# The first stage of a two-layer decoder trunk in another order: row parameters in one load, the first weights in two parts, work moved between ScalarE, VectorE and GpSimd

## The chip, the cores and the metric

The kernel runs on 1 core of one Trainium2 chip. Its time is device microseconds from start to end of one launch; lower is better. TensorE (PE in the profile) multiplies matrices, VectorE (DVE) and ScalarE (ACT) work element by element and reduce, GpSimd (POOL) does small operations, and SyncE (SP) issues nearly all loads. Each engine takes its instructions in the order in which the program gives them; a semaphore makes one wait for another.

## The reference

256 tokens of width 1024 go through two layers. Layer 0 mixes tokens with multi-head latent attention, layer 1 with block attention and a relative bias; a squared-ReLU MLP of width 4096 follows each. All is float32. The part that matters here is the entry of layer 0:

```python
h = rms_norm(x, attn_norm[0])
proj = h @ w_in                                   # 1024 -> 384 + 256 + 64
c_q, c_kv, k_pe = proj[..., :384], proj[..., 384:640], proj[..., 640:]
q = rms_norm(c_q, q_a_norm) @ w_uq                # 8 heads x (128 + 64)
kv = rms_norm(c_kv, kv_a_norm) @ w_ukv            # 8 heads x (128 + 128)
q_nope, k_nope = rms_norm(q[:128]), rms_norm(kv[:128])
q_pe = rope(rms_norm(q[128:]), cos, sin)          # cos, sin of positions * inv_freq
k_pe = rope(rms_norm(k_pe), cos, sin)
p = softmax(causal((q_nope . k_nope + q_pe . k_pe) / sqrt(192)))
```

## The kernel before

A float32 product is made of three products of operands that are split into a high and a low part: high by high, low by high, high by low. Weights come as units of up to 128 x 1024. `load_one` (L130) issues a unit's load on SP, `hi` (L140) casts its high part (`wh`) on ACT (L148), `lo` (L150) subtracts it on DVE for the low part (`wl`, L157). Seven units are split ahead at most (`RING`), and four raw tiles are in flight (`RAW`); `done` tells how far PE has come. The order of instructions on every engine is the order of the source: the program is scheduled by hand.

The first stage is the projection by `w_in`. Its eight units of 128 x 704 (slices k = 0 to 7, named `win0` to `win7`) each need a piece of x, transposed, in the tile `x`: `make_h` (L252) makes the high part `hTh` on ACT and the low part `hTl` on DVE. PE runs slices 0 to 5 as they come, into four PSUM tiles (`latk` for the key and value latent of 256 + 64 columns, `latq` for the query latent of 384, one of each for the two token blocks), and then `lat_end` (L421) does slices 6 and 7, one tile after the other, so that `ckv` can be copied and transposed (L452) while `latq` is still being summed. The units of `w_u` (tile `raw`) follow: keys `k0`, the rope part of the queries `p`, queries `q0`, values `v0`, then the second four heads. `hi()` and `lo()` calls stand between these steps.

Beside it run: the rope angles (`rope_angles`, L365) on POOL from positions `pos_q` and the row `rowc` (inverse frequencies and two gain rows), the sines on ACT (L437), the rope tables on POOL (`rope_tables`, L388); the sums of squares of the token rows `xs` on DVE (L462), which give the scales; the roots `hrs` of the norms on POOL (L245); rows multiplied by them on DVE (L339); the two rope products of `rope_rows` (L735), one on POOL (L739) and one on DVE (L740), and their sums (L746). `turn0` transposes the finished rows on PE (L347). An activation of one element loads ACT's table for Exp (L758) before it is needed in the softmax. The first `logits` end the stage.

SP's loads at the start go in this order: slice 0, x, slice 1, x, `pos_q`, `rowc` (one row broadcast to 128 partitions), slice 2, x, slice 3 and so on, two units of `w_u`, then both halves of `xs`.

Of the kernel before, what the change touches and what calls it, by code (L numbers as in the profile page):

```python
# [59 lines left out]
def trunk(ctx: ExitStack, tc: tile.TileContext, A, out):  # L60
# [304 lines left out]
    def rope_angles(eng):  # L365
        eng.tensor_copy(posf, pos_q)
        for t in range(NT):
            eng.tensor_scalar(ang[:, t], rowc[:, :HALF], posf[:, t:t + 1], None, op0=OP.mult)
        for j, shift in enumerate((0.25, 0.0)):
            kk = mla.tile([P, NT, HALF], F32, name=f"kk{j}")  # L370
            eng.tensor_scalar(kk, ang, 1.0 / TWO_PI, shift, op0=OP.mult, op1=OP.add)
            eng.tensor_scalar(kk, kk, MAGIC, None, op0=OP.add)  # L372
            eng.tensor_scalar(kk, kk, MAGIC, None, op0=OP.subtract)  # L373
            rr = mla.tile([P, NT, HALF], F32, name=f"rr{j}")
            pr = mla.tile([P, NT, HALF], F32, name=f"pr{j}")
            src = ang
            for c in (C1, C2, C3):
# [2 lines left out]
                src = rr  # L380
            if j == 0:
                eng.tensor_scalar(rr, rr, TWO_PI / 4, None, op0=OP.add)
            eng.tensor_scalar(rr, rr, 3.1415925, -3.1415925, op0=OP.min, op1=OP.max)  # L383
            angles.append(rr)
# [741 lines left out]
```

## Time and profile before

| | |
|---|---|
| median of 3 runs | 581.11 us (579.84 to 581.11) |
| the profiled execution | 581.29 us |
| its span, first to last instruction | 579.5 us |
| PE busy | 567.9 us (98%) |
| DVE busy | 406.6 us (70%) |
| ACT busy | 307.0 us (53%) |
| POOL busy | 115.8 us (20%) |
| read from HBM | 97.79 MB, 171 GB/s over the span |

The shares are means over the whole span. The change lies in the first 52 us, in which all engines wait for one another; after that PE works nearly without a break. A row of a timeline gives the start in us from the span's start, the duration (of several instructions of a kind together), the engine, the line of the source, the operation, the tiles written and read, and in brackets the idle time before it with what ended it.

### The profile page before, as it was taken

The page shows a single profiled execution, that of the slowest core. Times are in us where ns is not written, and L with a number is a line of the kernel's source. Part 1 is how long each engine was busy: PE and PEld are TensorE (multiplying, and loading weights), DVE is VectorE, ACT ScalarE, POOL GpSimd, SP SyncE. Part 2 cuts the span into 40 slices and gives each one's busy share as a digit, 9 for nine tenths or more (in the row PEclk, how much of TensorE's full clock was granted, in tenths as well). Part 3 has the DMA queues.
Part 4 walks back from the last instruction along what each step waited for, and adds up shares of the span by engine and source line. Part 5 has one row for each costly group of instructions (what it writes and reads, how often), then busy time and mean ns, then how long its engine had stood idle before and what let it go on. Part 6 is the DMA issues. An engine that isn't in the chain of part 4 may idle for free.

```text
span 579.5 us, 10767 instructions
## 1 busy us (share of the span) xinstructions
PE 567.9 (98%) x4346; PEld 541.0 (93%) x4346; DVE 406.6 (70%) x646; ACT 307.0 (53%) x492; POOL 115.8 (20%) x119
## 2 busy tenths in 40 slices
PE   7899999999999999999999999999999999999997
PEld 5767999999999999999988888999999999999996
DVE  5696877678899987786648456776778554756641
ACT  5787775655433364643545555756664433555420
POOL 5884100022122200024324100000131222000100
PEclk9998999999999999999999999999999999999999
DMA  7732535555655656575654554345466666465630
GB/s 282 287 92 74 178 112 151 190 186 170 206 167 157 187 168 208 159 235 185 202 177 126 191 187 127 133 146 163 152 189 199 204 183 184 149 210 163 237 125 28
DMA packets 29265, 99.54 MB, mean 172 GB/s; under 512 B 4032, under 2 KB 4672, under 8 KB 29216
## 3 DMA queue, kind: packets, MB, share of 16 engines
q1 hardware_dynamic: 28736, 97.92, 52.9%
q0 software_dynamic: 336, 0.92, 0.4%
q8 instruction: 34, 0.56, 0.4%
q14 instruction: 15, 0.12, 0.1%
q10 hardware_dynamic: 144, 0.02, 0.0%
HBM read 97.79 MB, written 1.05 MB: 171 GB/s over the span
## 4 chain that ended last, share of the span: by engine, by line
PE 92%; POOL 4%; DVE 1%; DMA 1%; issue 1%; SPq 0%; ACT 0%; POOLq 0%
PE ps L84 90%; POOL hrs L245 1%; PE ps L347 1%; PE ps L544 1%; DMA rowc<-in_rowc 1%; POOL pr L378 1%; POOL rr L379 1%; POOL t L739 0%; POOL kk L373 0%; POOL kk L372 0%; DVE sqj L462 0%; DVE cqT L469 0%; DVE wl L157 0%; POOL scl L245 0%; POOL rr L383 0%
## 5 line engine op out<-in xcount | busy, mean ns | idle before, releaser
L148 ACT CAST wh<-raw 128x1024 fp32r<-128x1024 f32 x177 | 183.5, 1047 | 111.5 <-DMA raw<-in_w_out_mlp 58.3
L157 DVE TENSOR_TENSOR wl<-raw,wh 128x1024 fp32r<-128x1024 f32 x177 | 228.1, 1318 | 8.8 <-ACT wh L148 8.6
L84 PE MATMUL ps<-a,wh 128*128 128x256 f32 x1024 | 183.5, 280 | 0.0
L84 PEld LDWEIGHTS ps<-a,wh 128*128 128x128 f32 x1024 | 157.2, 188 | 0.0
L84 PE MATMUL ps<-hTh,wh 128*128 128x256 f32 x512 | 143.8, 281 | 0.0
L84 PE MATMUL ps<-hTh,wl 128*128 128x256 f32 x512 | 143.1, 279 | 0.0
L84 PE MATMUL ps<-a,wl 128*128 128x256 f32 x512 | 142.9, 279 | 0.0
L84 PE MATMUL ps<-hTl,wh 128*128 128x256 f32 x512 | 142.8, 279 | 0.0
L84 PEld LDWEIGHTS ps<-hTh,wh 128*128 128x128 f32 x512 | 96.2, 188 | 0.1
L84 PEld LDWEIGHTS ps<-hTl,wh 128*128 128x128 f32 x512 | 96.0, 188 | 0.0
L84 PEld LDWEIGHTS ps<-hTh,wl 128*128 128x128 f32 x512 | 95.9, 187 | 0.1
L84 PEld LDWEIGHTS ps<-a,wl 128*128 128x128 f32 x512 | 95.8, 187 | 0.0
L84 PE MATMUL ps<-aT,wh 128*128 128x256 f32 x256 | 51.0, 289 | 0.0
L84 PE MATMUL ps<-wh,hTh 128*128 128x512 f32 (+2 forms) x128 | 45.9, 387 | 1.9 <-ACT wh L148 1.7
L909 POOL TENSOR_TENSOR x<-t,x 128x256 f32<-128x256 f32 x16 | 26.4, 1649 | 94.7 <-DVE t L907 94.7
L84 PE MATMUL ps<-wh,hTl 128*128 128x512 f32 (+2 forms) x128 | 44.6, 376 | 0.0
L84 PE MATMUL ps<-wl,hTh 128*128 128x512 f32 (+2 forms) x128 | 44.6, 376 | 0.0
L873 DVE SCALAR_TENSOR_TENSOR t<-ps,t 128x512 f32<-128x512 f32 (+1 forms) x34 | 22.4, 658 | 28.0 <-ACT t L871 28.0
L907 DVE TENSOR_TENSOR t<-ps,scale 128x256 f32<-128x256 f32 x32 | 13.5, 421 | 38.9 <-PE ps L84 38.9
L84 PEld LDWEIGHTS ps<-aT,wh 128*128 128x128 f32 x256 | 40.5, 188 | 0.2
L876 DVE TENSOR_TENSOR a<-t,a 128x512 fp32r<-128x512 f32 (+1 forms) x34 | 22.5, 661 | 22.5 <-ACT a L875 22.5
L245 POOL TENSOR_TENSOR hrs<-hss,mhalf 128x4 f32<-128x4 f32 (+1 forms) x18 | 24.9, 1390 | 65.8 <-DVE hss L322 48.9
(157 smaller groups left out, 653.1 us busy)
## 6 DMA issues: line engine op xcount, KB each, us to landing
raw<-in_w_in_mlp SPq DMA_DIRECT2D x64, 512.0 KB, 3.9
raw<-in_w_out_mlp SPq DMA_DIRECT2D x64, 512.0 KB, 3.8
raw<-in_w_qkv SPq DMA_DIRECT2D x24, 512.0 KB, 3.8
raw<-in_w_u SPq DMA_DIRECT2D x8, 512.0 KB, 6.1
win<-in_w_in SPq DMA_DIRECT2D x8, 352.0 KB, 5.2
raw<-in_w_o0a SPq DMA_DIRECT2D x4, 512.0 KB, 3.6
raw<-in_w_o0b SPq DMA_DIRECT2D x4, 512.0 KB, 3.4
raw<-in_w_o1a SPq DMA_DIRECT2D x4, 512.0 KB, 4.0
```

What stands on the lines that cost most here:

```text
L84: nc.tensor.matmul(o, a, b, start=start, stop=stop)
L148: (eng.copy if eng is nc.scalar else eng.tensor_copy)(his[i][:, :w], raws[i][:, :w])
L157: eng.tensor_sub(los[i][:, :w], raws[i][:, :w], f32(his[i][:, :w]))
L245: nc.gpsimd.tensor_tensor(dst, t, mhalf[:, :n].rearrange("p (a b) -> p a b", b=t.shape[-1]) if len(t.shape) == 3 else mhalf[:, :n], op=OP.pow)
L347: nc.tensor.transpose(pt[:, i * P:(i + 1) * P], yf[:, i * P:(i + 1) * P], ident)
L378: eng.tensor_scalar(pr, kk, c, None, op0=OP.mult)
L379: eng.tensor_sub(rr, src, pr)
L544: nc.tensor.transpose(pt[:, i * P:(i + 1) * P], self.p[:, i * P:(i + 1) * P], ident)
L873: nc.vector.scalar_tensor_tensor(sq, src, 0.0, rl, op0=OP.max, op1=OP.mult)
L876: nc.vector.tensor_sub(al, sq, f32(ah))
L907: nc.vector.tensor_tensor(y, o, scale, op=OP.mult)
L909: nc.gpsimd.tensor_add(x[:, d], y, x[:, d])
```

## The change

It changes the order of the first stage and the engines of a few operations. The two small loads become one: `rowp`, 162 words for each of 128 partitions, holds the row parameters already repeated, and the two positions of that partition. It is loaded after slice 3. Slice 0 is loaded in two parts, first the 320 columns of `latk`, then the 384 of `latq`; DVE casts the first part, ACT the second, and PE runs slice 0 as six products of 320 columns and then six of 384. The first half of `xs` is loaded before the units of `w_u`, the second after two of them. The sum of squares of the first half goes from DVE to ACT, ahead of the cast of slice 7. Of the angles, the second set (j = 1) goes from POOL to DVE, with a fused multiply and subtract, two steps at a time after the low parts of slices 3 to 6. The sines and rope tables come after the second copy of `cq`. `hi` and `lo` of three units move up by a step. Exp's table load moves from behind the latents to behind the first key transposition, the rope product of L739 goes from POOL to DVE, and the second `rope_rows` moves behind it.

```diff
+RC = HALF + 2 * PE_D
@@ load_one
-        nc.sync.dma_start(raw[:, :n], src)
+        c = slice(QR if i == 0 else 0, n)
+        nc.sync.dma_start(raw[:, c], src[:, c])
@@
-    pos_q = const.tile([P, NT], I32)
-    rowc = const.tile([P, HALF + 2 * PE_D], F32)
+    rowp = const.tile([P, RC + NT], I32)
+    rowc, pos_q = f32(rowp[:, :RC]), rowp[:, RC:]
@@
-        if k == 1:
-            nc.sync.dma_start(pos_q, A["pos_col"])
-            nc.sync.dma_start(rowc, A["rowc"].to_broadcast([P, HALF + 2 * PE_D]))
-    for t in range(NT):
-        load_one()
-    for t in range(NT):
-        nc.sync.dma_start(xs[:, t], A["x_tok"][t])
+        if k == 0:
+            nc.sync.dma_start(raws[0][:, :QR], units[0][0][:, :QR])
+        if k == 3:
+            nc.sync.dma_start(rowp, A["rowp"])
+    nc.sync.dma_start(xs[:, 0], A["x_tok"][0])
+    load_one()
+    load_one()
+    nc.sync.dma_start(xs[:, 1], A["x_tok"][1])
     load_raw()
@@ rope_angles, now for one j
+        eng = (nc.gpsimd, nc.vector)[j]
...
+        def less(src, c):
+            if j:
+                eng.scalar_tensor_tensor(rr, kk, -c, src, op0=OP.mult, op1=OP.add)
+            else:
                 eng.tensor_scalar(pr, kk, c, None, op0=OP.mult)
                 eng.tensor_sub(rr, src, pr)
...
-    rope_angles(nc.gpsimd)
+    rope_turns()
+    for step in rope_angles(0):
+        step()
+    sine = rope_angles(1)
+    win_parts = (slice(QR, QR + KVR + PE_D), slice(0, QR))
     for k in range(KD):
         if k == 0:
-            hi(1, nc.vector)
+            his.append(wsp.tile([P, 1024], F32R, name="wh", tag="wh"))
+            los.append(wsp.tile([P, 1024], F32R, name="wl", tag="wl"))
+            nc.vector.tensor_copy(his[0][:, win_parts[0]], raws[0][:, win_parts[0]])
             make_h(k, "attn0")
+            nc.scalar.copy(his[0][:, win_parts[1]], raws[0][:, win_parts[1]])
+            for c in win_parts:
+                nc.vector.tensor_sub(los[0][:, c], raws[0][:, c], f32(his[0][:, c]))
         else:
             make_h(k, "attn0")
             hi()
-        lo()
+            lo()
+        if 3 <= k < 7:
+            for step in sine[2 * (k - 3):2 * (k - 2)]:
+                step()
@@ the slices
         done(k)
+        if k == 0:
+            sq_sum(nc.scalar, 0, 0, xs[:, 0])
         if k < 2:
             hi()
             lo()
-        if k == 1:
-            for j in range(2):
-                nc.scalar.activation(trig[:, j], angles[j], AF.Sin)
-            rope_tables(nc.gpsimd)
@@ after the latents
     latents(ckvT, [ptk[0][:, i * S:(i + 1) * S] for i in range(2)], "kva")
+    sq_sum(nc.vector, 0, 1, xs[:, 1])
     lat_end(latq[1], 0, 1)
     nc.scalar.copy(cq[:, 1], latq[1])
-    for t in range(NT):
-        sq_sum(nc.vector, 0, t, xs[:, t])
+    for j in range(2):
+        nc.scalar.activation(trig[:, j], angles[j], AF.Sin)
+    rope_tables(nc.gpsimd)
     done(KD - 1)
@@ rope_rows
-        nc.gpsimd.tensor_mul(n.m1, n.y, ropeq[:, t, 1:2, :].to_broadcast([P, H, PE_D]))
+        nc.vector.tensor_mul(n.m1, n.y, ropeq[:, t, 1:2, :].to_broadcast([P, H, PE_D]))
@@
     lat_turn(ptq, cq, 0, 3)
+    hi()
+    lo()
     sq_sum(nc.scalar, 1, 1, ckv[:, 1, :KVR])
     sq_sum(nc.scalar, 2, 1, ckv[:, 1, KVR:])
-    hi()
...
-    lo()
-    nc.scalar.activation(warm, warm, AF.Exp)
     proj0("k0", 1)
@@
     post0("q0", 0, on_act=True)
+    hi()
+    lo()
     rows0("p", 1)
     proj0("q0", 1)
     post0("q0", 1, on_act=True)
-    rope_rows(1)
-    hi()
-    lo()
     rope_sum(0)
     turn0("k0", 0)
+    nc.scalar.activation(warm, warm, AF.Exp)
     proj0("v0", 0)
     rows0("q0", 0)
     turn0("k0", 1)
+    rope_rows(1)
     post0("v0", 0)
```

SP's queue from the start, before (each row an issue; the tile numbers tell the loads apart):

```order
L137 DMA win0_101<-in_w_in 128x704
L202 DMA x_81<-in_xT 128x256
L137 DMA win1_104<-in_w_in 128x704
L202 DMA x_81<-in_xT 128x256
L204 DMA pos_q_83<-in_pos_col 128x2
L205 DMA rowc_84<-in_rowc 128x160
L137 DMA win2_109<-in_w_in 128x704
L202 DMA x_81<-in_xT 128x512
```

The same queue in the changed kernel:

```order
L139 DMA win0_100<-in_w_in 128x320
L204 DMA x_81<-in_xT 128x256
L206 DMA win0_100<-in_w_in 128x384
L139 DMA win1_104<-in_w_in 128x704
L204 DMA x_81<-in_xT 128x256
L139 DMA win2_107<-in_w_in 128x704
L204 DMA x_81<-in_xT 128x512
L139 DMA win3_110<-in_w_in 128x704
L208 DMA rowp_83<-in_rowp 128x162
```

Slice 2 and the x tiles 2 and 3 now stand ahead of the row parameters, and slice 0 takes two issues.

ACT from the cast of slice 7 to the second copy of cq, before (`raw_124` and `raw_126` are the first two units of `w_u`):

```order
L148 CAST wh_257<-win7_122 128x704
L148 CAST wh_273<-raw_124 128x1024
L437 ACTIVATE trig_162<-rr0_174 128x64
L437 ACTIVATE trig_162<-rr1_188 128x64
L473 COPY ckv_344<-ps_243 128x320
L148 CAST wh_363<-raw_126 128x1024
L460 ACTIVATE sqj0_347,ssl_346<-ckv_344 128x256
L460 ACTIVATE sqj0_347,ssl_346<-ckv_344 128x64
L483 COPY cq_345<-ps_241 128x384
L467 ACTIVATE ckvT0_340<-ps_371,gains_82 128x256 x2
L487 COPY cq_345<-ps_242 128x384
```

ACT at the same place in the changed kernel:

```order
L455 ACTIVATE sqj0_244,ssl_243<-xs_84 128x1024
L150 CAST wh_259<-win7_121 128x704
L150 CAST wh_275<-raw_124 128x1024
L500 COPY ckv_333<-ps_241 128x320
L150 CAST wh_349<-raw_126 128x1024
L455 ACTIVATE sqj0_244,ssl_243<-ckv_333 128x256
L455 ACTIVATE sqj0_244,ssl_243<-ckv_333 128x64
L510 COPY cq_334<-ps_239 128x384
L494 ACTIVATE ckvT0_329<-ps_357,gains_82 128x256 x2
L515 COPY cq_334<-ps_240 128x384
L517 ACTIVATE trig_161<-rr0_170 128x64
L517 ACTIVATE trig_161<-rr1_184 128x64
```

The squares of `xs` stand ahead of slice 7, and the two sines behind the second copy of cq instead of ahead of the copy of ckv.

DVE from the first rope rows to the second rope sum, before (`t2` tiles are rows, `ropeq` the rope table, `wl` a low part):

```order
L339 TENSOR_TENSOR t2_536<-ps_490,hrs_504 128x512
L740 TENSOR_TENSOR t2_538<-t2_536,ropeq_163 128x512
L334 TENSOR_SCALAR hss_553<-hss_553,epsm_440 128x4
L339 TENSOR_TENSOR t2_561<-ps_509,hrs_523 128x512
L334 TENSOR_SCALAR hss_574<-hss_574,epsm_440 128x4
L740 TENSOR_TENSOR t2_582<-t2_561,ropeq_163 128x512
L157 TENSOR_TENSOR wl_588<-raw_369,wh_586 128x1024
L746 TENSOR_TENSOR t2_592<-t2_538,t2_539 128x8x32 x2
L339 TENSOR_TENSOR t2_608<-ps_542,hrs_558 128x512
L339 TENSOR_TENSOR t2_624<-ps_563,hrs_579 128x512
L746 TENSOR_TENSOR t2_626<-t2_582,t2_583 128x8x32 x2
```

DVE at the same place in the changed kernel:

```order
L342 TENSOR_TENSOR t2_533<-ps_487,hrs_501 128x512
L768 TENSOR_TENSOR t2_536<-t2_533,ropeq_162 128x512
L769 TENSOR_TENSOR t2_535<-t2_533,ropeq_162 128x512
L337 TENSOR_SCALAR hss_550<-hss_550,epsm_437 128x4
L159 TENSOR_TENSOR wl_560<-raw_355,wh_558 128x1024
L342 TENSOR_TENSOR t2_564<-ps_506,hrs_520 128x512
L337 TENSOR_SCALAR hss_577<-hss_577,epsm_437 128x4
L775 TENSOR_TENSOR t2_585<-t2_535,t2_536 128x8x32 x2
L342 TENSOR_TENSOR t2_602<-ps_539,hrs_555 128x512
L768 TENSOR_TENSOR t2_611<-t2_564,ropeq_162 128x512
L769 TENSOR_TENSOR t2_610<-t2_564,ropeq_162 128x512
L342 TENSOR_TENSOR t2_622<-ps_566,hrs_582 128x512
```

The two rope products of L768 are new on this engine, the low part stands ahead of the second rope rows, and the second pair of products behind the first rows of q.

## Rows read from the trace of the kernel before

**Rows 1.** Two stretches: us, busy time (instructions) by engine, granted clock, DMA share, GB/s.

```profile
core 0: us, PE busy (x) PEld busy (x) DVE busy (x) ACT busy (x) POOL busy (x), PEclk, DMA share, GB/s
0.00:51.00 51.00, 43.59 (x217) 35.06 (x218) 37.35 (x67) 34.50 (x86) 38.91 (x65) 0.97 0.57 200
51.00:577.00 526.00, 524.31 (x4130) 505.99 (x4130) 369.27 (x580) 272.49 (x407) 76.94 (x54) 1.00 0.54 170
```

**Rows 2.** Timeline of PE: start, duration, line, operation, [idle before <- released by].

```profile
10.96 0.91 PE L84 MATMUL ps<-wh,hTh 128*128 128x320 f32 x4 [1.72 <-ACT wh L148]
...
18.75 0.45 PE L84 MATMUL ps<-wh,hTh 128*128 128x320 f32 x2
...
22.79 0.41 PE L452 MATMUL ps<-ident,ckv 128*128 128x128 f32 x2 [2.12 <-ACT ckv L473]
...
44.37 0.73 PE L84 MATMUL ps<-wl,ckvT 128*128 128x512 f32 x2 [1.69 <-DVE wl L157]
...
46.07 0.90 PE L347 MATMUL ps<-ident,t 128*128 128x128 f32 x4 [0.30 <-DVE t L339]
...
50.38 0.39 PE L84 MATMUL ps<-k,q 128*128 128x128 f32 x2
```

**Rows 3.** One stretch, columns as in rows 1.

```profile
46.00:50.00 4.00, 3.93 (x15) 3.28 (x16) 2.72 (x5) 2.11 (x7) 2.99 (x3) 0.57 0.29 110
```

**Rows 4.** Timeline of ACT, columns as in rows 2.

```profile
9.73 0.51 ACT L254 ACTIVATE hTh<-x,gains 128x256 fp32r<-128x256 f32 x1 [2.80 <-DMA x<-in_xT]
...
16.20 0.77 ACT L148 CAST wh<-win 128x704 fp32r<-128x704 f32 x1
...
22.08 0.26 ACT L437 ACTIVATE trig<-rr 128x64 f32<-128x64 f32 x1 [3.91 <-POOL rr L383]
...
25.57 0.48 ACT L487 COPY cq<-ps 128x384 f32<-128x384 f32 x1
...
28.93 1.28 ACT L758 ACT_TABLE_LOAD   x1
```

**Rows 5.** Two stretches of the loads, columns as in rows 1.

```profile
5.00:7.00 2.00, 1.99 (x12) 1.99 (x12) 1.79 (x4) 1.18 (x2) 0.00 (x0) 1.00 0.34 68
9.00:10.00 1.00, 0.25 (x2) 0.00 (x0) 0.00 (x0) 0.27 (x1) 0.75 (x3) 1.00 1.04 415
```

**Rows 6.** Issues of xs: on SP's timeline; then count, KB each, median us to landing.

```profile
11.55 0.99 SPq L209 DMA_DIRECT2D xs<-in_x_tok  x2
...
xs<-in_x_tok SPq DMA_DIRECT2D x2, 512.0 KB, 8.5
```

**Rows 7.** Timeline of POOL, columns as in rows 2.

```profile
23.46 0.47 POOL L395 TENSOR_TENSOR ropek<-rowc,trig 128x128 f32<-128x128 f32 x1
...
26.54 2.42 POOL L402 TENSOR_SCALAR gqk<-gains 128x1 f32<-128x1 f32 x2
29.00 0.56 POOL L695 MEMSET kpT<- 128x256 f32 x2
31.78 1.04 POOL L245 TENSOR_TENSOR scl<-msl,mhalf 128x4 f32<-128x4 f32 x1 [2.21 <-DVE msl L766]
...
41.43 1.81 POOL L739 TENSOR_TENSOR t<-t,ropeq 128x512 f32<-128x512 f32 x1
43.20 2.98 POOL L245 TENSOR_TENSOR hrs<-hss,mhalf 128x4 f32<-128x4 f32 x2
```

**Rows 8.** Timeline of DVE, columns as in rows 2.

```profile
11.75 0.55 DVE L255 SCALAR_TENSOR_TENSOR hTl<-x,gains,hTh 128x256 fp32r<-128x256 f32 x1
...
18.11 1.25 DVE L157 TENSOR_TENSOR wl<-raw,wh 128x1024 fp32r<-128x1024 f32 x1
...
39.05 0.68 DVE L339 TENSOR_TENSOR t<-ps,hrs 128x512 f32<-128x512 f32 x1
...
42.01 2.30 DVE L157 TENSOR_TENSOR wl<-raw,wh 128x1024 fp32r<-128x1024 f32 x1
44.24 0.75 DVE L746 TENSOR_TENSOR t<-t,t 128x256 f32<-128x256 f32 x2
...
48.27 1.22 DVE L157 TENSOR_TENSOR wl<-raw,wh 128x1024 fp32r<-128x1024 f32 x1
```

More of the change, by code (lines that the diff above doesn't have):

```diff
@@ L363, in trunk, with rope_turns, rope_angles @@
     angles = []
-    def rope_angles(eng):
-        eng.tensor_copy(posf, pos_q)
+    def rope_turns():
+        nc.gpsimd.tensor_copy(posf, pos_q)
         for t in range(NT):
[L368 to L377, printed above, removed]
+            nc.gpsimd.tensor_scalar(ang[:, t], rowc[:, :HALF], posf[:, t:t + 1], None, op0=OP.mult)
+    def rope_angles(j):
+        eng = (nc.gpsimd, nc.vector)[j]
+        kk = mla.tile([P, NT, HALF], F32, name=f"kk{j}")
+        rr = mla.tile([P, NT, HALF], F32, name=f"rr{j}")
+        angles.append(rr)
+        steps = [lambda: eng.tensor_scalar(kk, ang, 1.0 / TWO_PI, (0.25, 0.0)[j], op0=OP.mult, op1=OP.add),
+                 lambda: eng.tensor_scalar(kk, kk, MAGIC, None, op0=OP.add),
+                 lambda: eng.tensor_scalar(kk, kk, MAGIC, None, op0=OP.subtract)]
+        pr = mla.tile([P, NT, HALF], F32, name=f"pr{j}")
+        def less(src, c):
+            if j:
+                eng.scalar_tensor_tensor(rr, kk, -c, src, op0=OP.mult, op1=OP.add)
+            else:
                 eng.tensor_scalar(pr, kk, c, None, op0=OP.mult)
                 eng.tensor_sub(rr, src, pr)
[L380 to L384, printed above, removed]
+        steps += [lambda: less(ang, C1), lambda: less(rr, C2), lambda: less(rr, C3)]
+        if j == 0:
+            steps.append(lambda: eng.tensor_scalar(rr, rr, TWO_PI / 4, None, op0=OP.add))
+        steps.append(lambda: eng.tensor_scalar(rr, rr, 3.1415925, -3.1415925, op0=OP.min, op1=OP.max))
+        return steps
     gsc = mla.tile([P, 3, PE_D], F32)
@@ L424, in lat_end, with sq_sum @@
                 lat_mm(o, g, t, k, i)
-    for k in range(KD - 2):
-        for i in range(3):
-            for t in range(NT):
-                lat_mm(latk[t], 1, t, k, i)
-                lat_mm(latq[t], 0, t, k, i)
+    ssl = small.tile([P, 4, NT], F32, name="ssl", bufs=1)
+    sqj = [early.tile([P, D], F32, name=f"sqj{i}") for i in range(2)]
+    def sq_sum(eng, i, t, src):
+        w = src.shape[-1]
+        if eng is nc.scalar:
+            nc.scalar.activation(sqj[0][:, :w], src, AF.Square, accum_out=ssl[:, i, t:t + 1])
+        else:
+            nc.vector.tensor_tensor_reduce(out=sqj[1][:, :w], in0=src, in1=src, op0=OP.mult, op1=OP.add,
+                                           scale=1.0, scalar=0.0, accum_out=ssl[:, i, t:t + 1])
+    for k in range(KD - 2):
+        if k == 0:
+            for g, lat in ((1, latk), (0, latq)):
+                for i in range(3):
+                    for t in range(NT):
+                        lat_mm(lat[t], g, t, k, i)
+        else:
+            for i in range(3):
+                for t in range(NT):
+                    lat_mm(latk[t], 1, t, k, i)
+                    lat_mm(latq[t], 0, t, k, i)
         done(k)
+        if k == 0:
+            sq_sum(nc.scalar, 0, 0, xs[:, 0])
         if k < 2:
@@ L452, in lat_turn @@
             nc.tensor.transpose(o, src[:, t, i * P:(i + 1) * P], ident)
-    ssl = small.tile([P, 4, NT], F32, name="ssl", bufs=1)
-    sqj = [early.tile([P, D], F32, name=f"sqj{i}") for i in range(2)]
-    def sq_sum(eng, i, t, src):
-        w = src.shape[-1]
-        if eng is nc.scalar:
-            nc.scalar.activation(sqj[0][:, :w], src, AF.Square, accum_out=ssl[:, i, t:t + 1])
-        else:
-            nc.vector.tensor_tensor_reduce(out=sqj[1][:, :w], in0=src, in1=src, op0=OP.mult, op1=OP.add,
-                                           scale=1.0, scalar=0.0, accum_out=ssl[:, i, t:t + 1])
     def latents(dst, srcs, g, i0=0):
@@ L1100 @@
         "gains": np.ascontiguousarray(np.concatenate(cols, axis=1)),
[L1101 to L1102 removed]
+        "rowp": rowp,
         "pos_row": np.ascontiguousarray(pos[None]),
```

5 lines of the change are left out of this document (2 added, 3 removed).

## Prediction

> **What bounds the kernel now.** I read the busy shares first, as a table of two stretches. From 51 us to 577 us TensorE (PE) is idle for 526.00 - 524.31 = 1.69 us; in the first 51 us it is idle for 7.41 us [rows 1]. Time can be gained only where PE stands idle or runs slowly, and that is at the start. So whatever makes PE reach the first attention head earlier is kept to the end, and nothing that the change does can gain much elsewhere. The second view is PE's timeline of those 51 us, with the idle time before each instruction and what released it [rows 2]. Four waits stand there:
>
> - 1.72 us before the third slice of the first projection (10.96), released by ACT's cast of the weights;
> - 2.12 us before the transposition of ckv (22.79), released by ACT's copy of ckv;
> - 1.69 us at 44.37, released by DVE's low part of a weight;
> - 0.30 us at 46.07, released by DVE's normalised rows.
>
> The first logits start at 50.38. A fifth loss is not idle time: from 46 to 50 us the granted clock is 0.57 in the mean, so PE ran at its lower level (1.2 GHz instead of 2.4) for most of it, after the idle time at 42.7 to 44.4. That costs 4 x 0.43 = 1.72 us [rows 3]. The two earlier gaps are as long, and no such fall followed them.
>
> The reference for the sum is the profiled execution itself: 581.29 us, 579.5 us of it span. The median of the timed runs is 581.11 us, so a gain counted in the profile may be taken from either.
>
> **Part 1: the loads at the start (row parameters later, first unit in two parts).** ACT's wait before the third slice is 2.80 us for x, which landed at 9.73 [rows 4]. Between 5 and 7 us the DMA engines moved 68 GB/s at a share of 0.34, between 9 and 10 us 415 GB/s at 1.04 [rows 5]. What SP's queue has at that place are the two small loads, of pos_q and of rowc. The 136 KB of those 2 us would take 0.33 us at 415 GB/s, so 1.67 us are lost there. In the new order, x's third load and the weights of slice 3 go ahead of the row parameters; 83 KB no longer stand in front either (0.20 us). So that x lands at 9.73 - 1.67 - 0.20 = 7.86. From landing to PE's start the trace has 10.96 - 9.73 = 1.23 us, so the third slice can start at 9.09. PE ended the second slice at 10.96 - 1.72 = 9.24 and will end it 0.2 us sooner, since slice 0 needs half the weight to begin. Gain: 10.96 - 9.09 = 1.87 us. What the merged load costs where it now stands no row shows. At best its bytes take 0.20 us; at worst it stalls the queue for 1.87 us like the old pair, which then delays x's later loads. These have slack, because PE takes 1.95 us for a slice (four between 10.96 and 18.75) and its 491 KB take 1.2 us at 415 GB/s, so of the 1.67 us some 1.2 would reach PE. I take the low end, since it is one load of 648-byte rows where there were two, one of them with 8-byte rows; the range keeps 1.2 us.
>
> **Part 2: Exp's load, the sines and the row sum on ACT.** The 2.12 us before 22.79 come from order on ACT: the copy of ckv stood behind the second sine, which waited 3.91 us for POOL's angles [rows 4]. The sines now stand behind the second copy of cq, so this wait goes. In its place something else is late: ACT now squares xs[0] ahead of the cast of slice 7, and this needs xs[0] in SBUF. The two xs loads were issued from 11.55 on, with a median of 8.5 us to landing [rows 6], so they landed around 20.05, the first about 0.6 sooner (half of the 1.26 us that its bytes take). The first one now goes ahead of two 512 KB loads (1.05 MB, 2.53 us), and all is 1.87 us sooner: about 15.0, and 15.7 without the 0.6. I take 15.4. ACT's cast of slice 7 took 0.77 us for a width of 704 [rows 4]; the squares are 1024 wide, so 1.1 us by width and 0.1 for reading the sum. The cast of slice 7 then runs from 16.6 to 17.4 (at 16.20 before). PE is free for it at 18.75 - 1.87 = 16.88. It waits about 0.5 us there and an estimated 0.2 more for the low part. Sum up to the transposition of ckv: 1.87 + 2.12 - 0.7 = 3.3 us gained; it starts at 19.5.
>
> The steps of the second angle (eight small instructions, an estimate of 0.2 us each by DVE's small operations) go to DVE between slices 3 and 6. There DVE takes 1.27 us for a slice (five between 11.75 and 18.11 [rows 8]) and PE 1.95, so two more steps a slice are hidden. Without that slack they would cost 1.6 us. Exp's table load (1.28 us at 28.93) moves to behind the first copy of k. What it stood before, the squares of k's projection, feeds the POOL chain of part 3, which is late for another reason; what stands behind it now is the second copy of k and those of v. I count nothing; if one of these copies is late, it is by at most the 1.28 us. DVE's row sum of xs[0] leaves the engine; I count nothing for that either, since DVE has to wait for POOL behind it.
>
> **Part 3: from the latents to the logits.** Here a chain over POOL and DVE ends last, and it moves less than PE. POOL's rope tables need the sines. These now follow the second copy of cq (done at 25.57 + 0.48 in the trace, 3.3 us sooner: 22.75) and end at 23.2. In the trace POOL took from 23.46 to 29.56 for the tables, the two gain products (2.42 us) and the clearing of kpT [rows 7]. Put behind 23.2 that ends at 29.3, where the next POOL step, the scales, started at 31.78 after an idle 2.21 us. If the gain products are not held up by DVE's sums it ends at 28.0. I take 28.7: the chain is 3.1 us sooner, not 3.3. From there the trace has 41.43 - 31.78 = 9.65 us to the end of the key sums, so 38.4. Then come the roots for q, 2.98 us for two, without the rope product of 1.81 us that stood before them: 41.4 (46.18 before).
>
> DVE starts the rope rows when POOL's first root for them is there: 39.05 in the trace, 3.1 us sooner now, 35.95. Behind it stand, up to the last rope sum, eight operations 512 wide (four rows, four products: 0.66 from start to start, 5.3), a low part (1.15), two pairs of sums (0.75 each, 1.4) and two small ones (0.4): 8.3 us [rows 8]. That ends at 44.25; with PE's transposition (0.45) the logits start at 44.65, 5.7 us sooner than at 50.38. Counted from PE's side: 1.72 + 2.12 + 1.69 + 0.30 + 1.72 + 0.15 (the earlier third slice) are removed, 7.7 us; new waits are 0.7 in front of slice 7 and 1.3 around 40 to 44 us, where PE waits for rope sums and rows.
>
> In this stretch DVE's low part that took 1.22 us elsewhere took 2.30 us beside POOL's rope product of 1.81 us [rows 7, 8]. The change takes that product off POOL and gives DVE two more of about 0.69 us, as wide as the rope rows (0.68). The Trainium skill, page "SBUF — State Buffer", section "SBUF: two separate sides", speaks against counting this as free: VectorE with two SBUF inputs and a GpSimd operation that reads SBUF take turns at one shared port pair, and whoever comes second waits for the whole instruction of the other. The 2.30 us agree with it. By that rule POOL's roots for q now wait behind DVE's products, up to 0.69 us each, and the logits would be up to 1.4 us later than in the sum.
>
> **Forecast:** 581.29 - 5.7 = 575.6 us, chance 0.50, its own range 574.4 to 577.0 (the bounds of 28.0 and 29.3 on POOL, 1.2 us of the row load).
>
> **Rivals.**
> - *The clock falls again, or the POOL and DVE chain is longer* (0.25). In the sum PE still idles some 1.3 us in pieces between 39 and 44 us; in the trace 1.99 us of idle time stood before the fall. For it: the fall came just there. Against: the pieces are shorter, and gaps of 1.72 and 2.12 us drew none. Price 1.72 us: 577.3. Two roots of POOL each waiting for a DVE product of 0.69 us, as DVE's low part waited for POOL's product (2.30 us against 1.22), cost 1.4: 577.0.
> - *The front end gives half of it back* (0.13): the row load stalls the queue (1.2) and xs[0] lands 2 us late. ACT's cast is then late by as much: 575.6 + 3.2 = 578.8.
> - *ACT's queue stands behind xs[0]* and the kernel is slower (0.07). ACT takes its work in order, so each us that xs[0] lands after 15.4 is one more for slice 7, for the copies of ckv and cq, for the sines and so for the whole chain. The gain of 5.7 is gone when it lands at 21.1, or at 19.4 if the clock falls in the long wait. For it: xs landed about 20 in the trace. Against: two big loads no longer stand before it. At 21.5 with the fall: 583.4.
> - *PE is early but the heads are not* (0.05): DVE and ACT can't follow after 44.65 and PE waits there for what it gained: 581. Against: DVE and ACT are busy 70% and 52% from 51 us on [rows 1], and they get the same shift.
>
> **How the numbers follow.** About 0.3% (1.7 us) is what a measurement of this kernel can tell from no change. Faster than that, below 579.4: 0.50 + 0.25 + 0.10 of the half gain = 0.85. Within it: 0.03 + 0.05 + 0.01 = 0.09. Slower: 0.06. The range leaves out some 0.06 below 573.9 (a gain over 7.4, nearly all waits gone) and some 0.14 above 579.4.
>
> **What would show it.** Right: no DMA dip below 100 GB/s between 5 and 7 us; third slice near 9.1; ckv transposed near 19.5; POOL's scales near 28.7; logits near 44.7; clock 1.0 throughout. Wrong: ACT's squares of xs[0] begin after 17; the clock falls below 1.0 anywhere; DVE waits for the angles; PE's idle time after 51 us exceeds 2 us.

## The result and the profile after

The changed kernel takes 575.44 us (median of 4 runs, 575.16 to 575.54), the kernel before on the same chip 580.48 us (579.6 to 581.11). The ratio is 0.9911, its 95% interval 0.9892 to 0.993. 575.6 us was predicted. In the profiled executions the span went from 579.5 to 573.4 us, 6.1 us less, and the first logits start 5.96 us sooner. From the logits to the end it is 528.98 us, 529.12 before, so behind them nothing but the start has moved.

By the medians the gain is 5.0 us, by the profiled executions (581.29 and 575.54 us) it is 5.75. The difference lies in the kernel before, whose executions differ in the mean granted clock. Of 40 beside the experiments, 9 had 0.999 or 1.0 and took 579.38 to 579.90 us; 31 had 0.993 to 0.997 and took 579.67 to 582.96. The profiled one had 0.996, with the fall of [rows 3] in it. Ten executions of the changed kernel all had 0.998 to 1.0. Two executions of about 691 us at a clock of 0.754, one each of two kernels below, are left out of their medians.

In the table of stretches PE is idle for 2.37 us in the first 51 us, 7.41 before, and the clock is at its upper level. These rows answer to [rows 1, 3, 5]; the last one is the stretch in which the loads were thin. The second ends 2.4 us before the end of the span, about as far from it as the second of [rows 1], and PE is idle in it for 1.72 us, 1.69 before.

```profile
core 0: us, PE busy (x) PEld busy (x) DVE busy (x) ACT busy (x) POOL busy (x), PEclk, DMA share, GB/s
0.00:51.00 51.00, 48.63 (x250) 39.64 (x251) 40.96 (x89) 41.88 (x111) 33.53 (x54) 1.00 0.61 209
...
45.00:571.00 526.00, 524.28 (x4131) 505.96 (x4130) 369.89 (x581) 272.51 (x407) 77.94 (x55) 1.00 0.54 170
...
46.00:50.00 4.00, 4.00 (x25) 3.44 (x24) 2.87 (x14) 4.00 (x14) 1.01 (x2) 1.00 0.41 131
...
5.00:7.00 2.00, 2.00 (x12) 1.91 (x10) 0.57 (x2) 0.86 (x2) 0.00 (x0) 1.00 0.99 282
```

PE's timeline of the changed kernel answers to [rows 2]. PE waits a little for ACT's casts before slices 1, 2 and 7; from the transposition of ckv to the logits it is idle for less than 0.1 us.

```profile
7.87 0.91 PE L85 MATMUL ps<-wh,hTh 128*128 128x320 f32 x4 [0.64 <-ACT wh L150]
...
10.28 0.91 PE L85 MATMUL ps<-wh,hTh 128*128 128x320 f32 x4 [0.22 <-ACT wh L150]
...
18.53 0.41 PE L85 MATMUL ps<-wh,hTh 128*128 128x320 f32 x1 [0.16 <-ACT wh L150]
...
20.58 0.38 PE L490 MATMUL ps<-ident,ckv 128*128 128x128 f32 x2
...
40.93 1.18 PE L350 MATMUL ps<-ident,t 128*128 128x128 f32 x8
...
44.42 0.40 PE L85 MATMUL ps<-k,q 128*128 128x128 f32 x2
```

So the 5.96 us have two parts. The transposition of ckv comes 22.79 - 20.58 = 2.21 us sooner, and the stretch from there to the logits is 23.84 us instead of 27.59, which is 3.75 us less.

ACT, POOL and DVE of the changed kernel answer to [rows 4, 7, 8]. On ACT, watch x's third landing, the squares of xs[0] ahead of slice 7, and the sines, which no longer wait:

```profile
9.05 0.51 ACT L257 ACTIVATE hTh<-x,gains 128x256 fp32r<-128x256 f32 x1 [1.23 <-DMA x<-in_xT]
...
16.66 1.06 ACT L455 ACTIVATE sqj<-xs 128x1024 f32<-128x1024 f32 x1 [0.58 <-DMA xs<-in_x_tok]
...
17.71 0.76 ACT L150 CAST wh<-win 128x704 fp32r<-128x704 f32 x1
...
23.70 0.40 ACT L517 ACTIVATE trig<-rr 128x64 f32<-128x64 f32 x2
...
37.31 1.28 ACT L840 ACT_TABLE_LOAD   x1
```

On POOL, the tables, the scales, the key sums (2.26 us for two, 0.88 before, first fence) and the roots for q (1.99 us for two, 2.98 in [rows 7]):

```profile
40.59 0.88 POOL L800 TENSOR_TENSOR t<-t 128x128 f32<-128x128 f32 x2
```

```profile
24.04 0.46 POOL L406 TENSOR_TENSOR ropek<-rowp,trig 128x128 f32<-128x128 f32 x1 [1.28 <-ACT trig L517]
...
29.30 1.04 POOL L248 TENSOR_TENSOR scl<-msl,mhalf 128x4 f32<-128x4 f32 x1
...
37.45 2.26 POOL L828 TENSOR_TENSOR t<-t 128x128 f32<-128x128 f32 x2
39.67 1.99 POOL L248 TENSOR_TENSOR hrs<-hss,mhalf 128x4 f32<-128x4 f32 x2
```

On DVE, the angles' first step, the rope rows, a low part at 1.21 us where [rows 8] has 2.30, and the last rope sum:

```profile
12.56 0.20 DVE L379 TENSOR_SCALAR kk<-ang 128x64 f32<-128x64 f32 x1 [0.18 <-POOL ang L371]
...
35.90 0.68 DVE L342 TENSOR_TENSOR t<-ps,hrs 128x512 f32<-128x512 f32 x1
...
38.17 1.21 DVE L159 TENSOR_TENSOR wl<-raw,wh 128x1024 fp32r<-128x1024 f32 x1
...
43.12 0.75 DVE L775 TENSOR_TENSOR t<-t,t 128x256 f32<-128x256 f32 x2
```

### The profile page after: what moved, and what is told of

It is laid out like the page before. It is cut to its first block, busy times and chain, and to the rows that moved or that the text cites. A ratio compares the mean times of both kernels' runs of the same rounds, so it can differ in the third digit from the quotient of the medians.

```text
span 573.4 us, 10762 instructions
## 1 busy us (share of the span) xinstructions
PE 566.9 (99%) x4346; PEld 540.6 (94%) x4346; DVE 406.8 (71%) x654; ACT 308.4 (54%) x495; POOL 109.5 (19%) x107
## 4 chain that ended last, share of the span: by engine, by line
PE 96%; DMA 2%; SPq 1%; DVE 0%; issue 0%; ACT 0%
PE ps L85 93%; PE ps L350 1%; DMA xs<-in_x_tok 1%; DMA win<-in_w_in 1%; PE ps L573 1%; SPq L204 0%; SPq L139 0%; PE ps L490 0%; DVE wl L159 0%; ACT wh L150 0%; DVE t L936 0%; DVE t L1002 0%; SPq L206 0%; ACT sqj L455 0%; PE ps L855 0%
## 5 line engine op out<-in xcount | busy, mean ns | idle before, releaser
L904 ACT CAST a<-t 128x512 fp32r<-128x512 f32 (+1 forms) x34 | 20.2, 595 | 32.8 <-DVE t L902 32.8
```

The source lines that it names most:

```text
L904: nc.scalar.copy(ah, sq)
```

## The experiments

Each takes the changed kernel and puts back one of its parts, or goes on from it. They ran on three chips; the kernel before had medians of 580.88 to 581.22 us beside them. The changed kernel itself, run a second time beside those with the angle on POOL, Exp's load early and the last row of the table, had 575.41 us. "Stretch" is the time from ckv's transposition to the logits, read from PE's timeline of each; where the start of the program scatters, it doesn't. What a time holds beyond the span is 1.80 to 1.95 us in six of these kernels and 2.06 to 2.19 in the others and the changed one, so 0.1 to 0.4 us of a difference of medians can lie outside the span.

| put back, or added | median us | to 575.4 | ratio to before, 95% | ckv T | logits | stretch |
|---|---|---|---|---|---|---|
| nothing (changed kernel) | 575.44, 575.41 | 0 | 0.9911 [0.9892, 0.993], 0.9912 [0.9896, 0.9927] | 20.58, 20.46 | 44.42, 44.29 | 23.84, 23.83 |
| slice 0 in one load | 574.71 | -0.7 | 0.9901 [0.9884, 0.9919] | 20.43 | 44.27 | 23.84 |
| two row loads, early | 577.09 | +1.7 | 0.9953 [0.9934, 0.9971] | 21.87 | 45.72 | 23.85 |
| sines before ckv's copy | 575.45 | 0.0 | 0.9918 [0.9904, 0.9932] | 21.49 | 44.99 | 23.50 |
| rope product on POOL | 576.55 | +1.1 | 0.9932 [0.9919, 0.9945] | 20.32 | 45.19 | 24.87 |
| low part later | 576.69 | +1.3 | 0.9927 [0.9908, 0.9947] | 20.57 | 45.47 | 24.90 |
| both of these | 576.95 | +1.5 | 0.993 [0.9911, 0.9949] | 20.25 | 45.33 | 25.08 |
| row sum on DVE | 576.34 | +0.9 | 0.9919 [0.9895, 0.9942] | 20.47 | 45.56 | 25.09 |
| second angle on POOL | 579.61 | +4.2 | 0.9984 [0.9971, 0.9997] | 20.14 | 48.60 | 28.46 |
| Exp's load early | 576.74 | +1.3 | 0.9934 [0.9918, 0.995] | 20.55 | 45.99 | 25.44 |
| one load, cast first, sum on DVE | 575.33 | -0.1 | 0.9905 [0.9884, 0.9926] | 19.46 | 44.56 | 25.10 |
| one load, cast first, sum on ACT | 574.58 | -0.8 | 0.9896 [0.9879, 0.9914] | 19.89 | 43.73 | 23.84 |

**Slice 0 in one load.**

```diff
-        c = slice(QR if i == 0 else 0, n)
-        nc.sync.dma_start(raw[:, c], src[:, c])
+        nc.sync.dma_start(raw[:, :n], src)
```

(with the cast of slice 0 on DVE alone and its products in the old order)

> The changed kernel, with slice 0 loaded and split in one piece as before (PE's order of slice 0 as before too). Theory 'short rows': the two part loads of slice 0 (rows of 1280 and 1536 bytes instead of 2816) are why the DMA engines moved only 261 GB/s at a share of 0.95 between 3 and 7 us, and why x's third load landed at 9.05 and not at the 7.9 of the prediction. Then without them x's second load lands at about 5.7 (6.64 in the changed kernel), its third at 8.0 to 8.3, the third slice starts at 9.2 to 9.5 (10.28), ckv is transposed 0.5 to 1.0 us sooner (20.58), and the end comes 0.4 to 1.0 us sooner: 574.4 to 575.0. Rival 'the row load': rowp itself or the order of the x loads holds the queue, the rates between 3 and 7 us stay near 260 GB/s, and slice 0 only starts 0.2 to 0.5 us later: 575.4 to 575.9.

The time is in the first theory's range. Its route did not hold: x's second load landed at 7.21 us, not 5.7, and the third slice started at 10.47. In the stretches of 2 to 9 us of before, of the changed kernel and of this one (columns as in the first table), the loads ran at 259, 296 and 330 GB/s:

```profile
2.00:9.00 7.00, 6.79 (x31) 4.69 (x29) 3.19 (x5) 2.33 (x5) 1.84 (x5) 1.00 0.77 259
```

```profile
2.00:9.00 7.00, 6.36 (x26) 4.54 (x25) 3.15 (x6) 2.84 (x6) 0.54 (x2) 1.00 0.95 296
```

```profile
2.00:9.00 7.00, 5.50 (x22) 3.20 (x21) 2.88 (x5) 2.62 (x6) 0.55 (x2) 1.00 0.96 330
```

At nearly the same share the one load moves more. But ckv is transposed only 0.03 to 0.15 us sooner, and 0.7 us were measured; some 0.3 of it lie outside the span (1.81 us here, 2.14 in the changed kernel) and 0.35 behind the logits, and which part of the program gave them no row shows. So it is not shown that loading slice 0 in two parts costs 0.7.

**The row loads back.**

```diff
-        if k == 3:
-            nc.sync.dma_start(rowp, A["rowp"])
+        if k == 1:
+            nc.sync.dma_start(pos_q, A["pos_col"])
+            nc.sync.dma_start(rowc, A["rowc"].to_broadcast([P, RC]))
```

> The changed kernel, with the two small loads of positions and row parameters back behind slice 1 and the second x, in their old form. Theory 'two small loads stall the queue': the dip below 100 GB/s comes back between 5 and 8 us, x's third load lands 1.3 to 1.9 us later (9.05), PE's third slice starts near 11.8 (10.28), and since PE has no waits to absorb it before 44 us, the end comes 1.0 to 1.6 us later: 576.4 to 577.0. Rival 'the POOL and DVE chain decides': the angles start 2 us sooner on POOL, the chain over the rope tables is what ends last, and the time stays within 0.5 us of 575.4.

The theory held: x's third load landed at 10.78 us and PE's third slice waited, as its row shows; all of it reaches the logits, since the stretch is the same 23.85. In the trace that is 1.30 us. The median, just above the theory's range, has more in it: four executions at a mean clock of 0.999 or 1.0 took 576.25 to 577.09 us, three at 0.994 to 0.997 took 578.63 to 579.97. The edit undoes the place and the form of the loads together; what each is worth was not run.

```profile
12.01 0.91 PE L85 MATMUL ps<-wh,hTh 128*128 128x320 f32 x4 [1.97 <-ACT wh L150]
...
21.87 0.38 PE L491 MATMUL ps<-ident,ckv 128*128 128x128 f32 x2
...
45.72 0.40 PE L85 MATMUL ps<-k,q 128*128 128x128 f32 x2
```

**The sines back ahead of ckv's copy.**

```diff
+        if k == 1:
+            for j in range(2):
+                nc.scalar.activation(trig[:, j], angles[j], AF.Sin)
+            rope_tables(nc.gpsimd)
...
-    for j in range(2):
-        nc.scalar.activation(trig[:, j], angles[j], AF.Sin)
-    rope_tables(nc.gpsimd)
```

> The changed kernel, with the sines and the rope tables back ahead of the copy of ckv. Theory 'order on ACT': the copy of ckv again stands behind a sine that waits for POOL's angles, which end at 20.78; ckv is copied at about 21.1 (19.91) and transposed at 21.6 (20.58), PE waits 1.0 us there, and the end comes 0.8 to 1.2 us later, 576.2 to 576.6; the wait is shorter than the 2.12 us of the kernel before because the second angles no longer follow on POOL. Rival 'sooner tables pay it back': POOL starts the rope tables 1.3 us sooner (22.8 for 24.04) and the logits come at the same time: 575.3 to 575.7.

The rival's time was measured. ACT's timeline has the sines wait for POOL's first angle, and ckv's copy stands behind them; PE loses 0.92 us there and the stretch gives back 0.34.

```profile
20.63 0.40 ACT L479 ACTIVATE trig<-rr 128x64 f32<-128x64 f32 x2 [1.39 <-POOL rr L394]
20.94 0.41 ACT L504 COPY ckv<-ps 128x320 f32<-128x320 f32 x1
```

The logits of this profiled run (576.28 us) come 0.57 us later than in the changed kernel's, but the run was 0.8 above the median of this kernel (575.29 to 576.28), so where the median makes that up no trace shows. Moving the sines was at most a small gain by itself.

**The rope product back on POOL, the low part back, and both.** The first edit is one word (`nc.gpsimd.tensor_mul(n.m1, ...)`); the second:

```diff
-    hi()
-    lo()
     rows0("p", 1)
     proj0("q0", 1)
     post0("q0", 1, on_act=True)
+    rope_rows(1)
+    hi()
+    lo()
     rope_sum(0)
...
     turn0("k0", 1)
-    rope_rows(1)
```

> The changed kernel, with the rope product back on POOL, in the order of the changed kernel. Theory 'POOL's chain': the product stands on POOL before the roots of q and takes 1.3 to 1.8 us; DVE's low part beside it takes 2.3 us; the first rope sums and rows of q come 1 to 2 us later than at 40.04 and 40.71, PE waits 1.5 us or more at 40.9, and the end comes 1.2 to 3.4 us later (the upper end if the granted clock falls as in the kernel before): 576.6 to 578.8. Rival 'it is a swap at the shared port': DVE is relieved of 1.4 us and POOL burdened with as much, the two cancel: 575.2 to 575.8.

> The order of DVE's and ACT's steps around 36 to 44 us is put back as it was: both parts of the next weight (cast and low part) and the rope rows of the second token half stand behind the second pair of q's projection steps, so that DVE makes the low part after the two rope products instead of before the second rows. The products stay on DVE. Theory (the 1.69 us wait before the low part was a matter of order): PE waits 1.2 to 1.7 us for wl near 41 us again, the clock holds: 576.6 to 577.2; if the clock falls behind that wait as before, 1.7 more, 578.3 to 578.9. Rival (the wait came from the rope product on POOL, which held up the low part to 2.30 us, and the order did nothing): at most 0.3 of wait, 575.2 to 575.8.

> As the run with the old order, and the rope product is also back on POOL: the whole of the stretch from 36 to 44 us as it was before, with the earlier front end. Theory (two causes that add up): the 1.69 and 0.30 us waits come back, with the clock's fall to 0.57 over 4 us behind them (1.7): 1.99 + 1.72 = 3.7 us, 578.5 to 579.5. Rival A (the clock's fall belonged to where the gaps stood, with the earlier front end none comes): 577.2 to 577.8. Rival B (one wait, which either edit removes): as the product alone, 576.3 to 576.8.

Alone they cost 1.1 us, just under the first theory's 1.2, and 1.3, as the second had it. Together they cost 1.5, near rival B of the third text, not the sum. The timelines say why. With the product on POOL, DVE stands for it ahead of the first rope sums (first fence, DVE); the low part runs ahead of that product and takes 1.22 us, not the 2.3 of the theory. With the old order and the product on DVE, the low part takes 1.21 us but starts late (second, DVE); PE's row is in the third. With both, the low part takes 2.33 us beside POOL's product of 1.83, as in [rows 8], yet starts 1.57 us sooner (0.3 of it by the start), since DVE doesn't make the first products itself (fourth, DVE), so that PE waits 1.06 us (fifth).

```profile
40.36 0.76 DVE L775 TENSOR_TENSOR t<-t,t 128x256 f32<-128x256 f32 x2 [1.26 <-POOL t L768]
```

```profile
40.09 1.21 DVE L159 TENSOR_TENSOR wl<-raw,wh 128x1024 fp32r<-128x1024 f32 x1
```

```profile
41.36 0.73 PE L85 MATMUL ps<-wl,ckvT 128*128 128x512 f32 x2 [1.19 <-DVE wl L159]
```

```profile
38.52 2.33 DVE L159 TENSOR_TENSOR wl<-raw,wh 128x1024 fp32r<-128x1024 f32 x1
```

```profile
40.90 0.73 PE L85 MATMUL ps<-wl,ckvT 128*128 128x512 f32 x2 [1.06 <-DVE wl L159]
...
42.59 0.63 PE L350 MATMUL ps<-ident,t 128*128 128x128 f32 x4 [0.30 <-DVE t L342]
```

The clock stayed at 1.00 from 36 to 50 us in both kernels with the late low part. The 3.71 us that before lost here (1.99 of waits, 1.72 of clock) come back as only 1.2 to 1.5 when both edits are undone. The fall of the clock is part of the other 2.2 or more, and only some executions of before have it; what the other edits do for this stretch no run divides.

**The row sum of xs[0] back on DVE**, where both sums stood, ahead of the latents of cq:

```diff
-        if k == 0:
-            sq_sum(nc.scalar, 0, 0, xs[:, 0])
+    sq_sum(nc.vector, 0, 0, xs[:, 0])
     sq_sum(nc.vector, 0, 1, xs[:, 1])
```

> The row sum of the first half of x goes back from ACT to DVE, behind the latents of ckv, where both sums stood. Theory (the sum costs ACT 1.06 us in front of the cast of slice 7, of which PE waits 0.16): that wait goes, ckv is transposed 0.1 to 0.3 us sooner, and DVE hides its 1.1 us behind PE: 575.0 to 575.5. Rival (DVE is the late engine there, as its scales and rows feed POOL): the chain over POOL gets 0.5 to 1.1 us later, 575.8 to 576.6.

The rival's price came, at another place: not over POOL, but PE itself waits for the low part of cqT, which stands behind the two sums on DVE. That wait is 0.93 of the 1.25 us by which the stretch is longer.

```profile
28.44 1.29 PE L85 MATMUL ps<-wh,cqT 128*128 128x512 f32 x3 [0.93 <-DVE cqT L494]
```

**The second angle back on POOL.**

```diff
-        eng = (nc.gpsimd, nc.vector)[j]
+        eng = nc.gpsimd
```

(with its multiply and subtract as two instructions again, and all its steps behind the first angle's)

> The second angle goes back to POOL, behind the first; the sines stay behind the second copy of cq. Theory (the 2.12 us wait for ckv and POOL's late tables came from POOL making both angles, so DVE's share of them is what pays, not the place of the sines): POOL ends the second angle 6 to 7 us after the first, near 27; ACT stands at the second sine from 23.7 to 27, the rope tables start 3.0 to 3.5 us later, POOL's scales near 32.5, the logits 3.0 to 3.4 us later: 578.4 to 579.0, and 580.1 to 580.7 if the clock falls in the wait. Rival (the tables have slack, POOL catches up before the scales): 575.4 to 576.5.

The path is the theory's, and the time, 4.2 us more, lies between its two ranges. It is the dearest part of the change; what the engine, the fused step and the place of the steps are worth one by one was not run. ACT stands at the second sine; behind it stand the cast and the latents of cq, for which PE waits 2.17 us; POOL's scales start at 31.85. Two stretches of this execution then show the clock at 0.81 and 0.77, which is 4 x 0.19 + 4 x 0.23 = 1.68 us. With the waits of 2.17, 0.24 and 0.39 that makes 4.48 of the 4.62 by which the stretch is longer. But that is the account of one execution: three others had a mean clock of 1.0 and took 579.60 to 580.04 us, no less than most of the nine with 0.995 to 0.997 (579.32 to 581.46). The fall isn't on the path to the end, either: the chain that ended last, followed back in this trace, goes over POOL from 10.04 to 40.06 us, then over DVE, whose rope rows wait 1.56 us for POOL's root, and over PE only from 45.12 on. ACT's row, PE's, DVE's, and the table:

```profile
26.27 0.26 ACT L515 ACTIVATE trig<-rr 128x64 f32<-128x64 f32 x1 [2.76 <-POOL rr L394]
```

```profile
28.66 2.93 PE L85 MATMUL ps<-wh,cqT 128*128 128x512 f32 x6 [2.17 <-ACT cqT L492]
```

```profile
40.08 0.69 DVE L342 TENSOR_TENSOR t<-ps,hrs 128x512 f32<-128x512 f32 x1 [1.56 <-POOL hrs L248]
```

```profile
26.00:30.00 4.00, 1.82 (x6) 1.23 (x5) 2.22 (x4) 3.70 (x11) 3.68 (x9) 0.81 0.11 16
30.00:34.00 4.00, 4.00 (x15) 3.11 (x15) 3.79 (x13) 2.97 (x7) 3.78 (x9) 0.77 0.33 122
```

**Exp's table load back behind the latents of cq** (one line, moved).

> Exp's table load goes back to ACT's place behind the latents of cq, where it stands in front of the squares of k's projection. Theory (these squares have slack): 575.2 to 575.7. Rival (they feed the sums of which POOL makes its roots, and are 1.28 us late): 576.2 to 576.8.

The theory fell; the time is the rival's, the route only in part. ACT loads the table at 26.89 us in front of the squares of k; DVE then waits 0.77 us for the next cast and only 0.19 for the squares, and PE waits 0.42 and 0.39 us. The stretch is 1.60 us longer; no row names the other 0.8. ACT's row and DVE's:

```profile
26.89 1.28 ACT L787 ACT_TABLE_LOAD   x1
```

```profile
28.91 0.69 DVE L321 TENSOR_REDUCE hss<-t 128x4 f32<-128x512 f32 x1 [0.19 <-ACT t L320]
...
31.49 1.23 DVE L159 TENSOR_TENSOR wl<-raw,wh 128x1024 fp32r<-128x1024 f32 x1 [0.77 <-ACT wh L150]
```

**Two steps further, and the changed kernel again.** Both kernels have slice 0 in one load and ACT's cast of slice 1 and of the even slices ahead of x's high part; the first has the row sum on DVE, the second on ACT behind the cast of slice 7.

```diff
+            if k == 1 or k % 2 == 0:
+                hi()
+                make_h(k, "attn0")
+            else:
                 make_h(k, "attn0")
                 hi()
```

> Slice 0 in one load, x's first row sum on DVE, and for slice 1 and the even slices ACT casts the weights ahead of x's high part (the weights are issued first, x lands last there). Theory (of the 1.23 us from x's landing to PE's start the cast of 0.77 us can be done before): slice 1 starts at 7.7 us, not 8.44, later slices follow PE without a wait, ckv is transposed 0.7 to 0.8 us sooner than with one load alone (near 19.7), 573.8 to 574.4. Rival A (the chain over POOL and DVE sets the logits, PE waits near 40 us for what it gained): 574.5 to 575.0. Rival B (the weights of a slice land with or after x, so ACT stands behind them and x's high part gets later): slice 1 at 8.4 or later, 574.7 to 575.5.

> As the kernel with the cast ahead of x's high part, but the first row sum stays on ACT, now behind the cast of slice 7. Theory (that kernel lost 0.94 us again, since DVE's sum stood before the low part of cqT): no wait for cqT near 27.4, ckv transposed at 19.4 to 19.6, 23.84 us from there to the logits: 43.4, 574.0 to 574.4. Rival (the chain over POOL and DVE is late by what PE gained): PE waits 0.5 to 1.0 near 40, 574.8 to 575.4.

> The changed kernel itself, unchanged, beside the three others on the same chip, to compare them with. 575.2 to 575.8; slice 1 begins between 7.8 and 8.5 us, as in the runs with the same start, and the logits 36.5 us behind it.

The first one brought ckv to 19.46 us, 0.2 sooner than its theory had, and lost it at cqT, where PE waited 0.94 us, as in the kernel with the sum on DVE. Its 575.33 us is in rival B's range, but not by B's route, since slice 1 started at 6.99 us. DVE's timeline shows the two sums ahead of the low parts:

```profile
22.98 1.48 DVE L454 CUSTOM_DVE_ANT_0 sqj<-xs 128x1024 f32<-128x1024 f32 x1
...
24.50 1.23 DVE L454 CUSTOM_DVE_ANT_0 sqj<-xs 128x1024 f32<-128x1024 f32 x1
...
26.91 1.26 DVE L485 SCALAR_TENSOR_TENSOR cqT<-ps,gains,cqT 128x256 fp32r<-128x256 f32 x3
```

The second lost nothing: its ckv came at 19.89, 0.3 us later than expected, the stretch is 23.84, and 574.58 us (574.21 to 574.84, its theory had 574.0 to 574.4) is the fastest median of all, 0.8 below the changed kernel (575.3 to 575.66) on the same chip. Against the kernel with one load alone (574.71, not beside it) it can't be told apart. Its PE timeline:

```profile
19.89 0.38 PE L481 MATMUL ps<-ident,ckv 128*128 128x128 f32 x2
...
43.73 0.40 PE L85 MATMUL ps<-k,q 128*128 128x128 f32 x2
```

## Why the prediction was right, point by point

*The end of the sum: the right time, but not by the chain named.* The forecast took the logits from the chain over POOL and DVE, with PE waiting for it. That chain came about when it was forecast: scales at 29.30 (28.7 predicted), key sums done at 39.71 (38.4), rope rows at 35.90 (35.95), last rope sum done at 43.87 (44.25), logits at 44.42 (44.65). But the logits did not wait for it. PE is idle for less than 0.1 us from ckv's transposition to the logits, and when ckv comes at 19.89 (last row of the table), the chain's steps come sooner too (scales at 28.61) and the stretch is the same 23.84. The chain of work that ended last, which the profiler follows back from the end (start, duration, step), shows it too. In before it leads from the row parameters' load over POOL's two angles to ACT's copy of ckv, and later over POOL's scales:

```profile
3.05 5.07 DMA rowc<-in_rowc
...
22.24 0.42 ACT ckv L473
```

In the changed kernel it goes over xs[0], its squares and the cast and low part of slice 7, and then over PE alone to the logits and far beyond:

```profile
16.66 0.05 ACT sqj L455
...
17.81 0.68 ACT wh L150
...
18.51 0.90 DVE wl L159
...
19.46 1.29 PE ps L85 x7
```

On PE's side two errors cancel: it reached ckv 1.08 us late (20.58 for 19.5), and from there it took 23.84 us where the sum has 44.65 - 19.5 = 25.15, since the waits of 1.3 us between 40 and 44 did not come. So the 0.2 us between the forecast and the measured logits is in part luck. The reference helped too: 5.7 us were taken off an execution of 581.29 us, while the median beside the changed kernel was 580.48, and the medians are 5.0 apart.

*The third slice: wrong size.* A gain of 1.87 us was predicted and 0.68 measured. The step that failed is "the 136 KB of those 2 us would take 0.33 us at 415 GB/s, so 1.67 us are lost there". The dip went, but the loads in its place did not run at 415: 282 GB/s from 5 to 7 us at a share of 0.99. From 2 to 9 us the queue moved 7 x (296 - 259) = 259 KB more, by estimate 0.62 us at 415 GB/s and 0.87 at 296; x's third load gained 0.68 (9.73 to 9.05). Nine kernels here have the same loads at the start; x's third landed in them between 8.56 and 9.19, never at 7.86. PE's second slice did not end 0.2 us sooner either, but at 10.06 instead of 9.24, since x's second load landed at 6.64 (5.75 before); so the third could not have started at 9.09 even with x in time. What the merged load costs by itself no run shows; the old pair in its old place costs 1.3 us in the trace and 1.7 in the median.

*Slice 7 and ckv: 2.2 instead of 3.3.* The squares of xs[0] began at 16.66, not 15.4; 1.19 of these 1.26 us are what x's third load gained less than the 1.87 that the sum had carried over to them. The cast behind them began at 17.71. PE waited only 0.16 us there, since it came late itself. The wait of 2.12 went, as said. Its row named ACT and POOL's angles, and neither brings it back alone: with the sines early PE waits 0.92 us for ckv and the median stays; with the angle on POOL ckv is in time, and the 4.2 us are lost behind it, from cqT on. Both edits together were not run.

*"I count nothing": half right.* The angle's steps on DVE were hidden, as said (0.18 us of wait for them). The row sum and Exp's load were not free: undone, they cost 0.9 and 1.3 us. "DVE has to wait for POOL behind it" and "late for another reason", of POOL's chain, were read from the kernel before; in the changed one DVE's timeline names no wait from 24.1 to 44 us, and POOL's none from the first table at 24.04 to 41.66.

*The lock.* In the Trainium skill, page "SBUF — State Buffer", section "SBUF: two separate sides", VectorE with two SBUF inputs and a GpSimd operation that reads SBUF take turns at one port pair. The traces agree on both sides: DVE's low part takes 2.33 us beside POOL's product and 1.21 without it, and POOL's two key sums take 2.26 us beside DVE's second product and low part where they took 0.88. By that rule POOL's roots would have put the logits up to 1.4 us later; POOL's sums and roots together ended at 41.66 where the sum had 41.4. So the price showed in the sums, and the roots, which in before ran beside the low part of [rows 8], took 1.99 us instead of 2.98.

*The clock* held in all ten executions of the changed kernel (0.998 to 1.0 in the mean), so that rival fell. What draws a fall is less plain. In the traces, waits of 1.97 us (third slice, row loads put back) and of 1.06 to 1.19 us (low part) drew none, the one of 2.17 us before cqT did. But one and the same kernel falls in some executions and not in others: the kernel before (mean clocks of 0.993 to 1.0), that with the row loads put back (0.994 to 1.0) and that with the angle on POOL (0.995 to 1.0). The length of a gap alone doesn't tell. Of the other rivals, xs[0] did not cost the gain (16.66 us; the sum put the loss of all of it at 19.4 to 21.1), though the chain that ended last goes through it (with its squares on DVE, ckv is at 20.47 and gains at most 0.1), and the heads followed at once (PE's idle time behind them is the same).

*The signs.* The clock, the logits and the gone dip were as forecast, POOL's scales within 0.6 us; the third slice (10.28) and ckv (20.58) were not. Of the signs of being wrong, DVE did wait for the angles, but 0.18 us that the end does not show. PE's idle time after 51 us, up to 572, is 2.72 us, but only since that window reaches nearer to the end than the one of [rows 1]. The forecast's two ranges, 574.4 to 577.0 and 573.9 to 579.4, do not agree; 575.44 is in both.

*Not additive.* Seven parts put back one at a time cost 1.7 + 0.0 + 1.1 + 1.3 + 0.9 + 4.2 + 1.3 = 10.5 us; the whole change gained 5.0. In the changed kernel PE, DVE and POOL run from 24 to 41 us with hardly a wait, so one part made late mostly shows at once; that several parts hide the same wait, as the product and the low part do, is shown for that pair alone.

## What to carry to other kernels

Where several engines feed one, work out the end of every branch, and afterwards look which one the changed kernel waited for: here the total was right, and the branch that ended last was another than forecast. Look at more than one execution of the reference, as its profile may be the one with the fall of the clock. "Hidden behind another wait" holds only as long as that wait stands: when one change removes several waits, price each hidden edit against the kernel after, not the one before. Fill a dip in the loads at the rate that the loads there reach, not at the best rate of the trace.

## What the runs showed of the hardware

A full queue isn't a fast one: from 2 to 9 us the nine kernels that start with the changed kernel's loads (slice 0 in two parts) moved 280 to 306 GB/s at a share of 0.91 to 0.99, the three with slice 0 in one load 330 to 333 at 0.95 to 0.96. Neither is near the 415 of [rows 5]. Whether the shorter rows or the number of loads do it, no run divides.

The landing of a load isn't settled by what stands in front of it. x's second load was issued at 2.10 to 2.11 us behind the same three loads in before and in the three kernels with one load; it landed at 5.75 in before, at 7.21, 6.43 and 6.62 in the others. In before the two small loads came next. But that this is the reason is not shown: with the row loads put back the small ones come next too, and it landed at 6.62. Identical starts scatter as much: in the nine kernels x's second load landed between 6.11 and 7.28, and slice 1 started between 7.34 and 8.51. By ckv's transposition (20.14 to 20.58, the kernel with early sines aside) most of that scatter is gone.

PE's own time from ckv's transposition to the logits is 23.83 to 23.85 us in the five kernels without a wait there. Such a constant stretch shows a wait of half a microsecond that a single time may not: the executions of before spread over 3.6 us.
